# Second head's keys in the weight buffers, parked loads and half rows placed anew, first output norms one tile later: a two-layer hybrid trunk on one Trainium2 core

## The chip, the cores and the metric

One core of one Trainium2 chip runs the whole program. The metric is the device time in microseconds (us) from launch to end; the median of three runs of the kernel before is 3038.08 us, and the runs lie between 3037.23 and 3039.92. The traces come from one further execution, taken by the hardware profiler. Engines are named as in the profile: PE (TensorE matmul), DVE (VectorE), ACT (ScalarE), POOL (GpSimd), SP (SyncE, whose queue issues most of the DMAs).

## The reference, cut to what matters

Two layers run over 256 context tokens and then over 1024 latent tokens with the same weights. Each layer computes, in float32:

```
h  = rms_norm(x) * (1 + sc1) + sh1
p_pool, p_q, p_k, p_v, p_uv = split(h @ w_in)
y_a = multiscale_pool(p_pool) @ w_pool
y_b = for 4 heads: (softmax(q1 k1^T/8) - lam * softmax(q2 k2^T/8)) @ v, then rms_norm per head
y_c = chunked gating of p_uv
x  = x + g1 * (concat(y_a, y_b, y_c) @ w_out)
h2 = rms_norm(x) * (1 + sc2) + sh2
gate, up = split(h2 @ w_ffn_in)
x  = x + g2 * ((silu(gate) * up) @ w_ffn_out)
```

The modulations sh, sc and g are silu(cond) @ w_ada. Latent queries see 256 cached keys and 1024 own ones, so 1280 keys a head; context queries see the 256 context keys.

## The kernel before, in words

All 1280 tokens stand as three column chunks (`CH`): chunk 0 is the 256 context tokens, chunks 1 and 2 are 512 latent tokens each. A float32 product is made of three float32r matmuls, for which each operand is split into a rounded high part and a remainder: `split` (L107 to L109) casts on ACT and subtracts on DVE. Weights come from HBM by a DMA on SP's queue into a raw tile (`raw_slab`, L102 to L105, two buffers), and the two parts land in one of **four weight buffers** (`wtile`, L114). A list of loads in the order of use (`want`, `fetch`, `load_w`) says which weight comes next; `fetch(n)` issues loads and splits until n tiles are ready.

PE's order is the order of the program everywhere. The other engines' order is made by the framework's planner, with its own costs and priorities, so a load or a DVE instruction can be put earlier than its line; only the latent attention is ordered by hand on every engine (`man`, L917 to L1037).

**Latent attention** (L963 to L1036) goes through 32 query tiles of 128 tokens, j = 0 to 31, eight for each of the four heads, with three more turns to drain. A turn makes the two score products of tile j (`s0`, `s1`, L397), their row maxima on DVE (`m0`, `m1`, L401), the exponentials on ACT (`e0`, `e1`, L404), and the transposes (L932) and value products (L415) of earlier tiles. At the first tile of a head, `load_q` brings its queries and `load_kb` (L811 to L821) its keys: four tiles of 1280 columns, two DMAs each, all on SP's queue. The pool of these tiles has five buffers, so one tile of a new head can be loaded ahead and three have to wait for the last tile of the old head. In the first tile of a head (`new`, L999) the transposes and the first value product stand before the second score product, elsewhere they stand inside and behind it. Four of the coming output weights are fetched at j = 5, 8, 11 and 14 (L1033), each with one cast on ACT and one subtraction on DVE in the hand-written order. During head 0 the four weight buffers hold at first the query weights and then head 0's values (one buffer).

**The output product** (`w_out`, L1075) multiplies the mixed rows with the output weights. Its part for chunk 0 needs only what is ready; those for chunks 1 and 2 need the attention's rows scaled by their norms, which `mix_out` does (L1082): four multiplications on DVE (L433), four transposes on PE (L438), a copy on ACT and a subtraction on DVE. In the kernel before, two `mix_out` stand behind each of the four `w_out(0, m)` (L1089 to L1091).

**The FFN** multiplies the 22 slabs of `w_ffn_in` with chunks 1 and 2 as a two by two block product with seven instead of eight half products (`seven`, L1292). For five slabs (1 to 5, `PRE`) the first two of them are made beforehand, parked in HBM (`FS`), and read back by `kept` (L1285); `five` (L1330) makes the other five. Seven-product and five-product slabs alternate (`AFTER`, L42). The sums of weights that the scheme needs are made on POOL (L156 to L169). Between the products, `ada_after` issues half rows of `w_ada` (`ada_half`, L280): one DMA on SP's queue into one of two buffers, and two reductions on DVE (L286) placed behind a marked instruction. Tiles for copies (`cp`), for gates (`g`) and for half rows (`ra`) have three, three and two buffers.

The order at a five-product slab is

```
product(pa_, quarter(s24, 0), t2)
V.tensor_add(u2, p1, pa_)               # L1336
product(pc, quarter(s31, 1), t1)
V.tensor_add(u3, p1, pc)                # L1340
product(pa_, quarter(s31, 0), t3, False)
```

so PE's third product, which writes on into `pa_`, waits until L1336 has read it.

Of the kernel before, what the change touches and what calls it, by code (L numbers as in the profile page):

```python
# [19 lines left out]
P = 128  # L20
# [3 lines left out]
SEQ = 256  # L24
# [25 lines left out]
def build(tc, d):  # L50
# [13 lines left out]
    def nm(s):  # L64
        uid[0] += 1
        return f"{s}_{uid[0]}"
# [475 lines left out]
    for l in range(DEPTH):  # L542
# [265 lines left out]
        kx = ExitStack()  # L808
        kp = opened(kx, "kp", side="right")

        def load_kb(pool, h, k0, n, tag, bufs):  # L811
            kb = []
            for m in range(2):
                row = []
                for i in range(2):
                    t = pool.tile([P, n], F32R, tag=tag, bufs=bufs, name=nm("kb"))
                    for r in range(2):
                        ld(t[r * 64:(r + 1) * 64], KS[l][i, h, m * 64:(m + 1) * 64, k0:k0 + n])
                    row.append(t)
                kb.append(row)  # L820
            return kb  # L821
# [141 lines left out]
        for j in range(NQ + 3):  # L963
            if j < NQ:
                h, i = divmod(j, 8)
                if i == 0:
                    aq = load_q(h, SEQ)
                    kb = load_kb(kp, h, SEQ, NKEY, "kb", 5)
                    box = {}
                elif i % 2 == 0:  # L970
                    aq = aq_next
                if i % 2 and i < 7:
                    aq_next = load_q(h, SEQ + (i + 1) * P)
                if j == 2:
                    open_rest()
                if i == 0:
                    if j == 0:
                        wt = wp.tile([P, 2, 1024], F32R, tag="w", bufs=4, name=nm("vt"))
                        vt = [wt[:, x, :5 * P].bitcast(F32).rearrange("p (a e) -> p a e", e=P) for x in range(2)]
                    else:  # L980
                        vt = [boxes["bp"].tile([P, 5, P], F32, tag="vt", bufs=3, name=nm("vt")) for _ in range(2)]
                    box["vt"] = vt
                    hc = slice(h * P, (h + 1) * P)
                    for x, n, src in ((0, 2, d["cv"][l, :, hc]), (2, 3, VS[l][SEQ:SEQ + 3 * P, hc]),
                                      (5, 5, VS[l][SEQ + 3 * P:, hc])):
                        nc.gpsimd.dma_start(vt[x // 5][:, x % 5:x % 5 + n],
                                            src.rearrange("(a p) e -> p a e", p=P))
                if (j and i == 0) or j == 2:
                    box["o"] = boxes["bo"].tile([P, 8, P], F32, tag="o", bufs=NH - 1, name=nm("o")) \
                        if h < NH - 1 else op.tile([P, 8, P], F32, tag="o", name=nm("o"))  # L990
                    o_all.append(box["o"])
                if j > 2 and mix_ld:
                    c, y = mix_ld.pop(0)
                    t0, n = CH[c]
                    for x in range(2):
                        nc.gpsimd.dma_start(mix[c][:, x, (0, 1, 6, 7)[y]].bitcast(F32),
                                            MS[l].bitcast(F32)[x, y, :, t0:t0 + n])
                tiles[j] = dict(h=h, i=i, kb=kb, aq=aq, box=box, st=stt[:, h], E=[])
            new = j < NQ and j % 8 == 0 and j > 0  # L999
            piece(j, "s0")  # L1000
            piece(j, "m0")
            if j != 1 and j != 2:
                piece(j - 1, "e1")
            piece(j - 3, "v2")
            piece(j - 3, "out")
            piece(j - 2, "t0")
            piece(j - 2, "c0")
            if j != 1 and j != 2:
                piece(j - 1, "comb")
            if new or j >= NQ:  # L1010
                piece(j - 2, "t1")
                piece(j - 2, "c1")
                piece(j, "e0")
                piece(j - 2, "v0")
                piece(j, "s1")
                piece(j, "m1")
            else:
                piece(j, "s1")
                piece(j - 2, "c1")
                piece(j, "e0")  # L1020
                piece(j, "m1")
                piece(j - 2, "v0")
            piece(j - 2, "t2")
            piece(j - 2, "c2")
            piece(j - 2, "v1")
            if j < 2:
                late()
                piece(j, "e1")
                piece(j, "comb")
                late = qk_step(ws, True, 2, 2 + j, psum())  # L1030
            if j == 1:
                late()
            if j in (5, 8, 11, 14):  # L1033
                fetch(j // 3)
            if j in (3, 5):
                ctx_out(j // 2 - 1)  # L1036
        man.close()  # L1037
# [44 lines left out]
        def mix_out(c, h):  # L1082
# [2 lines left out]
            out_norm(l, o_all[h][:, b * 4:b * 4 + 4],  # L1085
                     mix[c][:, 0, 2 + h], mix[c][:, 1, 2 + h])

        ws = load_w(4)
        for m in range(4):  # L1089
            w_out(0, m, ws[m])  # L1090
            mix_out(1 + m // 2, 2 * (m % 2))  # L1091
            mix_out(1 + m // 2, 2 * (m % 2) + 1)
        ab.close()
        fa = ExitStack()
        ntb[0] = 3
# [39 lines left out]

        for c in (1, 2):
            for m in range(4):
                w_out(c, m, ws[m])
                if c == 2:
                    fetch(m + 1)  # L1140
                ada_halves(2)
# [150 lines left out]
        def seven(f, wg, pa_, p1, s24, wh, rest, more, ctx, lead):  # L1292
            first = not callable(rest)
            if lead:
                g1 = product2(wg, p1)
            product(pa_, quarter(s24, 0), t2, False)
            u2 = copied(pa_)
            if not lead:
                g1 = product2(wg, p1)
            if ctx:  # L1300
                pg = ctx_gate(wg)
            a21, s31 = (None, rest) if first else rest()
            pc = fpsum(512)
            product(pc, quarter(s31, 1), t1)
            product(pa_, quarter(s31, 0), t3, False)
            u3 = copied(pa_)
            nxt = product1(load_w(1, 1)[0]) if more else None
            mark = V.tensor_add(u3, u3, pc)
            if ctx:
                ada_after(mark, 1)  # L1310
            if ctx and not more:
                ctx_up((a21, wh), f, pg)
            product(pa_, wh, t4, False)
            mark = V.tensor_mul(g1, g1, pa_)  # L1314
            keep_ft(f, 1, g1)
            ada_after(mark, 1)
            if ctx and more:
                ctx_up((a21, wh), f, pg)
            fetch(1)
            product(pc, quarter(s24, 1), b22, False)  # L1320
            g2 = gtile()
            V.tensor_add(g2, u2, pc)
            S.activation(g2, g2, AF.Silu)
            mark = V.tensor_mul(g2, g2, u3)
            keep_ft(f, 2, g2)
            ada_after(mark, 1)
            return nxt


        def five(f):  # L1330
            s24, wh = load_w(1, 1)[0]
            p1, g1 = kept(f, 2, "cp"), kept(f, 1, "g")
            pa_, pc = fpsum(512), fpsum(512)
            product(pa_, quarter(s24, 0), t2)
            u2 = fpa.tile([P, 512], F32, tag="cp", bufs=3, name=nm("pc"))
            V.tensor_add(u2, p1, pa_)  # L1336
            s31 = load_w(1, 1)[0]
            product(pc, quarter(s31, 1), t1)
            u3 = fpa.tile([P, 512], F32, tag="cp", bufs=3, name=nm("pc"))
            V.tensor_add(u3, p1, pc)  # L1340
            product(pa_, quarter(s31, 0), t3, False)
            ada_after(V.tensor_add(u3, u3, pa_), 1)
            product(pc, quarter(s24, 1), b22, False)
            g2 = gtile()
            V.tensor_add(g2, u2, pc)
            S.activation(g2, g2, AF.Silu)
            V.tensor_mul(g2, g2, u3)
            keep_ft(f, 2, g2)
            fetch(1)
            product(pa_, quarter(wh, 0), t4, False)  # L1350
            V.tensor_add(p1, p1, pa_)
            V.tensor_mul(g1, g1, p1)
            keep_ft(f, 1, g1)

        s24, s31 = load_w(2, 2)
        seven(FIRST - 1, *product1(w[0]), s24, quarter(w[1], 1), s31, False, False, True)
        nxt = None
        for f, g in zip(AFTER, AFTER[1:] + (None,)):
            if f in PRE:
                five(f)  # L1360
                continue
            lead = nxt is None
            if lead:
                nxt = product1(load_w(1, 1)[0])
            s24, wh = load_w(1, 1)[0]

            def rest():
                return load_w(2, 2)

            nxt = seven(f, *nxt, s24, quarter(wh, 0), rest, g is not None and g not in PRE, f >= FIRST, lead)  # L1370
# [210 lines left out]
```

## Time and profile before

| | |
|---|---|
| median of three runs | 3038.08 us |
| the profiled execution's own time | 3045.66 us |
| its span, first to last instruction | 3043.9 us |
| PE busy | 2917.2 us, 96% of the span |
| DVE, ACT, POOL busy | 1997.3, 1110.9, 687.8 us |
| mean granted TensorE clock | 0.986 of full speed |

PE is the bound of nearly all of the span. What can be saved by a change that leaves the products as they are is the time in which PE waits or runs slower, so the places at which it waits are what is to be read. A time "[1.35 <-DMA kb<-KS]" behind an instruction of the trace is the engine's idle time before it and what ended it.

### The profile page before, as it was taken

The numbers are of one execution on the slowest core, as the hardware profiler recorded it, in microseconds if no ns is written. First come the engines' busy times: TensorE is split into PE (matmuls) and PEld (weight loads), VectorE is DVE, ScalarE is ACT, GpSimd is POOL, SyncE is SP. The second block draws the span as 40 slices with busy tenths as digits, with TensorE's granted clock in tenths as the row PEclk, the third lists the DMA queues.
The fourth block names the chain that finished last, engine by engine and source line by source line (L and its number), as shares of the span: only waits on it lengthen the run. The fifth ranks groups of instructions, "written<-read, shape, count | busy, mean of one in ns | idle before, by whom it ended". The sixth has DMA issues, their size and how long they took to land.

```text
span 3043.9 us, 41519 instructions
## 1 busy us (share of the span) xinstructions
PE 2917.2 (96%) x15800; PEld 2500.7 (82%) x15800; DVE 1997.3 (66%) x3221; ACT 1110.9 (36%) x1887; POOL 687.8 (23%) x756
## 2 busy tenths in 40 slices
PE   7999899999999999999989998999999999999997
PEld 4888788888778888888877887888878888888886
DVE  5777777666665554776768767766866533347767
ACT  4423577254222323211252236761632222231112
POOL 1222300035433332000112222000454433310002
PEclk9999999999999999999999999999999999999998
DMA  6476632533333233521235665424433322152211
GB/s 227 152 219 186 190 94 54 180 130 119 120 121 111 94 99 106 189 94 67 77 111 162 209 171 170 115 88 145 138 116 127 101 68 68 68 195 94 94 63 70
DMA packets 155959, 380.65 MB, mean 125 GB/s; under 512 B 20320, under 2 KB 52336, under 8 KB 155504
## 3 DMA queue, kind: packets, MB, share of 16 engines
q1 hardware_dynamic: 111232, 274.00, 28.6%
q0 software_dynamic: 44240, 103.84, 10.1%
q8 instruction: 124, 2.03, 0.3%
q14 instruction: 75, 0.61, 0.1%
q10 hardware_dynamic: 288, 0.16, 0.0%
HBM read 281.97 MB, written 95.95 MB: 124 GB/s over the span
## 4 chain that ended last, share of the span: by engine, by line
PE 78%; DVE 10%; DMA 4%; issue 3%; ACT 3%; POOL 1%; SPq 0%; DVEq 0%; POOLq 0%; ACTq 0%
PE f L217 33%; PE f L1242 24%; PE pa L217 6%; PE pa L457 4%; PE S L397 4%; PE ps L415 4%; PE ps L932 2%; DMA kb<-KS 2%; DVE w L109 1%; DVE ps L286 1%; DVE stt L401 1%; ACT E L404 1%; DVE ps L274 1%; ACT w L108 1%; DMA raw<-w_adaT 1%
## 5 line engine op out<-in xcount | busy, mean ns | idle before, releaser
L217 PE MATMUL f<-ft,w 128*128 128x512 f32 (+1 forms) x3168 | 615.0, 356 | 0.0
L217 PEld LDWEIGHTS f<-ft,w 128*128 128x128 f32 x3168 | 524.8, 190 | 86.8
L108 ACT CAST w<-raw 128x1024 fp32r<-128x1024 f32 x246 | 254.2, 1049 | 723.0 <-PE f L217 410.4
L1242 PE MATMUL f<-h,w 128*128 128x512 f32 x2112 | 506.9, 391 | 1.1 <-ACT pc L1190 1.1
L109 DVE TENSOR_TENSOR w<-raw,w 128x1024 fp32r<-128x1024 f32 x246 | 307.6, 1259 | 295.9 <-ACT w L108 295.5
L1242 PEld LDWEIGHTS f<-h,w 128*128 128x128 f32 x2112 | 392.8, 188 | 82.7 <-ACT pc L1190 1.9
L1072 DVE SCALAR_TENSOR_TENSOR x<-f,mod,x 128x512 f32<-128x512 f32 (+1 forms) x544 | 340.8, 653 | 168.8 <-PE f L217 165.1
L1242 PE MATMUL f<-T,w 128*128 128x512 f32 x1080 | 265.9, 395 | 19.7 <-DVE pc L1336 16.8
L1242 PEld LDWEIGHTS f<-T,w 128*128 128x128 f32 x1080 | 202.4, 188 | 69.9 <-DVE pc L1336 20.8
L217 PE MATMUL pa<-h,w 128*128 128x512 f32 (+1 forms) x1296 | 249.8, 353 | 0.8 <-DVE vn L635 0.8
L401 DVE TENSOR_REDUCE stt<-S 128x1 f32<-128x1280 f32 x128 | 189.8, 1487 | 76.1 <-PE S L397 76.1
L217 PEld LDWEIGHTS pa<-h,w 128*128 128x128 f32 x1296 | 212.6, 192 | 32.5 <-DVE vn L635 1.0
L316 POOL TENSOR_TENSOR nacc<-nacc,room 128x512 f32<-128x512 f32 (+1 forms) x45 | 51.3, 1140 | 799.1 <-ACT room L315 742.3
L457 PE MATMUL pa<-w,h 128*128 128x512 f32 x912 | 220.0, 399 | 11.2 <-DVE w L109 10.7
L217 PE MATMUL f<-mix,w 128*128 128x512 f32 (+1 forms) x1152 | 225.7, 356 | 0.0
L397 PE MATMUL S<-kb,aq 128*128 128x512 f32 (+1 forms) x768 | 198.9, 384 | 19.0 <-DMA kb<-KS 11.7
L457 PEld LDWEIGHTS pa<-w,h 128*128 128x128 f32 x912 | 172.9, 192 | 52.6 <-DVE w L109 8.7
L217 PEld LDWEIGHTS f<-mix,w 128*128 128x128 f32 x1152 | 190.9, 190 | 29.5
L1183 POOL DMA_DIRECT2D FS<-sg x132 | 73.1, 554 | 568.2 <-DVE sg L1314 227.8
L415 PE MATMUL ps<-vt,pt 128*128 128x128 f32 x1280 | 180.7, 282 | 5.9 <-ACT pt L938 5.9
L404 ACT ACTIVATE E<-S,stt 128x1280 f32<-128x1280 f32 x128 | 170.5, 1332 | 38.8 <-DVE stt L401 38.8
L217 PEld LDWEIGHTS f<-h,w 128*128 128x128 f32 x1392 | 172.7, 192 | 3.3
(230 smaller groups left out, 3928.0 us busy)
## 6 DMA issues: line engine op xcount, KB each, us to landing
raw<-w_fi SPq DMA_DIRECT2D x112, 512.0 KB, 3.7
ft<-FS SPq DMA_DIRECT2D x44, 640.0 KB, 5.1
ra<-w_adaT SPq DMA_DIRECT2D x96, 256.0 KB, 2.9
FS<-sg POOLq DMA_DIRECT2D x88, 256.0 KB, 2.3
raw<-w_fo SPq DMA_DIRECT2D x44, 512.0 KB, 5.3
kb<-KS SPq DMA_DIRECT2D x64, 320.0 KB, 6.4
raw<-w_adaT SPq DMA_DIRECT2D x32, 512.0 KB, 4.2
raw<-w_in SPq DMA_DIRECT2D x20, 512.0 KB, 3.6
```

What stands on the lines that cost most here:

```text
L108: S.copy(hi, src)
L109: V.tensor_sub(lo, src, hi.bitcast(F32))
L217: PE.matmul(ps, lhsT=a, rhs=b, start=(i == 0), stop=(i == n - 1))
L397: PE.matmul(ps[:, o:o + n], lhsT=aq[:, m, q0:q0 + P], rhs=kb[m][1 - p][:, o:o + n], start=(p == 0), stop=(p == 1))
L401: V.reduce_max(st[:, m:m + 1], ps[:, :nkey], axis=AX.X, negate=True)
L404: S.activation(E, ps[:, :nkey], AF.Exp, bias=st[:, m:m + 1], accum_out=st[:, 2 + m:3 + m])
L415: PE.matmul(o[:, :P], lhsT=pt[:, i * P:(i + 1) * P], rhs=vt(b + i), start=(b + i == 0), stop=(b + i == nk - 1))
L457: PE.matmul(ps, lhsT=a[:, y], rhs=wk[:, z], start=(k == 0 and x == 0), stop=(k == KD - 1 and x == 2))
L932: PE.transpose(T_["tp", b][:, x * P:(x + 1) * P], T_["E"][0][:, (4 * b + x) * P:(4 * b + x + 1) * P], ident)
L1072: V.scalar_tensor_tensor(xs[c][:, m], in0=ps, scalar=mods[l][:, g0 + m, COND[c]:COND[c] + 1], in1=xs[c][:, m], op0=ALU.mult, op1=ALU.add)
L1183: nc.gpsimd.dma_start(FS[l][f, :, t0:t0 + n], sg)
L1242: PE.matmul(ps, lhsT=y, rhs=z, start=(first and i == 0), stop=(i == 11), skip_group_check=not first)
```

## The change

The second head's keys (h = 1) take one tile from the keys' pool and three from the weight buffers. The fetches of the output weights move from j = 5, 8, 11, 14 to j = 25, 27, 29, 31. The `mix_out` pairs start behind `w_out(0, 1)` instead of `w_out(0, 0)`, and `w_out(1, 0)` is made before the last pair. In the FFN the parked values of a coming five-product slab are asked for inside the seven-product slab ahead of it (`keep_next`), the half row at the end of such a slab moves to the end of the five-product slab, and the first product of the next slab is made before the five-product slab's last product.

```diff
-        def load_kb(pool, h, k0, n, tag, bufs):
+        def load_kb(pool, h, k0, n, tag, bufs, own=4):
...
-                    t = pool.tile([P, n], F32R, tag=tag, bufs=bufs, name=nm("kb"))
+                    if 2 * m + i < own:
+                        t = pool.tile([P, n], F32R, tag=tag, bufs=bufs, name=nm("kb"))
+                    else:
+                        t = wtile().rearrange("p a b -> p (a b)")[:, :n]
...
-                    kb = load_kb(kp, h, SEQ, NKEY, "kb", 5)
+                    kb = load_kb(kp, h, SEQ, NKEY, "kb", 5, 1 if h == 1 else 4)
...
-            if j in (5, 8, 11, 14):
-                fetch(j // 3)
+            if 24 < j < 32 and j % 2:
+                fetch((j - 23) // 2)
...
+        left = [(c, h) for c in (1, 2) for h in range(NH)]
+
+        def mix_two():
+            for _ in range(min(2, len(left))):
+                mix_out(*left.pop(0))
+
         ws = load_w(4)
         for m in range(4):
             w_out(0, m, ws[m])
-            mix_out(1 + m // 2, 2 * (m % 2))
-            mix_out(1 + m // 2, 2 * (m % 2) + 1)
+            if m:
+                mix_two()
+        w_out(1, 0, ws[0])
+        mix_two()
         ab.close()
...
             for m in range(4):
-                w_out(c, m, ws[m])
+                if (c, m) != (1, 0):
+                    w_out(c, m, ws[m])
...
             if ctx and more:
                 ctx_up((a21, wh), f, pg)
+            if not more:
+                keep_next(f)
             fetch(1)
             product(pc, quarter(s24, 1), b22, False)
...
             keep_ft(f, 2, g2)
-            ada_after(mark, 1)
+            ada_after(mark, int(more))
             return nxt
+
+        parked = {}
+
+        def keep_next(f):
+            g = dict(zip((FIRST - 1,) + AFTER, AFTER)).get(f)
+            if g in PRE:
+                parked[g] = kept(g, 2, "cp"), kept(g, 1, "g")
...
-            p1, g1 = kept(f, 2, "cp"), kept(f, 1, "g")
+            p1, g1 = parked.pop(f)
...
             keep_ft(f, 2, g2)
-            fetch(1)
+            nxt = product1(load_w(1, 1)[0])
             product(pa_, quarter(wh, 0), t4, False)
             V.tensor_add(p1, p1, pa_)
-            V.tensor_mul(g1, g1, p1)
+            mark = V.tensor_mul(g1, g1, p1)
             keep_ft(f, 1, g1)
+            ada_after(mark, 1)
+            return nxt
...
             if f in PRE:
-                five(f)
+                nxt = five(f)
                 continue
```

## Rows read from the trace of the kernel before

**Rows 1.** The page: shares of the chain that ended last, by engine.

```profile
PE 78%; DVE 10%; DMA 4%; issue 3%; ACT 3%; POOL 1%; SPq 0%; DVEq 0%; POOLq 0%; ACTq 0%
```

**Rows 2.** Timeline of DVE, layer 0: start us, us, instruction [idle before, releaser].

```profile
368.55 1.49 DVE L401 TENSOR_REDUCE stt<-S 128x1 f32<-128x1280 f32 x1 [0.84 <-PE S L397]
...
393.50 1.49 DVE L401 TENSOR_REDUCE stt<-S 128x1 f32<-128x1280 f32 x1 [0.87 <-PE S L397]
...
423.70 1.48 DVE L401 TENSOR_REDUCE stt<-S 128x1 f32<-128x1280 f32 x1
...
445.46 1.49 DVE L401 TENSOR_REDUCE stt<-S 128x1 f32<-128x1280 f32 x1 [0.87 <-PE S L397]
...
494.55 1.49 DVE L401 TENSOR_REDUCE stt<-S 128x1 f32<-128x1280 f32 x1 [0.99 <-PE S L397]
...
523.06 1.49 DVE L401 TENSOR_REDUCE stt<-S 128x1 f32<-128x1280 f32 x1 [0.90 <-PE S L397]
```

**Rows 3.** The same timeline of DVE, layer 1.

```profile
1870.33 1.49 DVE L401 TENSOR_REDUCE stt<-S 128x1 f32<-128x1280 f32 x1 [0.82 <-PE S L397]
...
1891.19 1.49 DVE L401 TENSOR_REDUCE stt<-S 128x1 f32<-128x1280 f32 x1 [0.50 <-PE S L397]
...
1921.77 1.48 DVE L401 TENSOR_REDUCE stt<-S 128x1 f32<-128x1280 f32 x1
...
1941.58 1.49 DVE L401 TENSOR_REDUCE stt<-S 128x1 f32<-128x1280 f32 x1 [1.03 <-PE S L397]
```

**Rows 4.** Timeline of PE: head 1 in layer 0, head 2 in layer 1.

```profile
381.28 2.47 PE L397 MATMUL S<-kb,aq 128*128 128x512 f32 x6 [3.08 <-DMA kb<-KS]
...
1926.40 1.40 PE L397 MATMUL S<-kb,aq 128*128 128x512 f32 x6 [0.57 <-ACT pt L938]
...
1932.01 1.43 PE L397 MATMUL S<-kb,aq 128*128 128x512 f32 x6 [1.35 <-DMA kb<-KS]
```

**Rows 5.** Timeline of SP's queue, layer 0: the issues of head 1's keys.

```profile
360.60 11.47 SPq L100 DMA_DIRECT2D kb<-KS  x8
```

**Rows 6.** Timeline of PE: start of the output product, layer 0, then layer 1.

```profile
542.34 1.61 PE L438 MATMUL ps<-ident,o 128*128 128x128 f32 x8 [2.34 <-DVE o L433]
...
546.66 1.03 PE L438 MATMUL ps<-ident,o 128*128 128x128 f32 x8
...
2039.48 1.94 PE L438 MATMUL ps<-ident,o 128*128 128x128 f32 x8 [2.05 <-DVE o L433]
2041.07 3.91 PE L217 MATMUL f<-mix,w 128*128 128x256 f32 x24
```

**Rows 7.** Line L1336: who waited for it (total us, times).

```profile
  PE f L1242: 16.8, 9
```

**Rows 8.** Timeline of PE, third product of three of the five-product slabs.

```profile
860.38 4.30 PE L1242 MATMUL f<-T,w 128*128 128x512 f32 x12 [2.02 <-DVE pc L1336]
...
2398.55 3.06 PE L1242 MATMUL f<-T,w 128*128 128x512 f32 x12 [1.34 <-DVE pc L1336]
...
2437.41 3.04 PE L1242 MATMUL f<-T,w 128*128 128x512 f32 x12
```

**Rows 9.** Timeline of DVE about the first five-product slab, layer 0.

```profile
775.16 1.77 DVE L1324 TENSOR_TENSOR sg<-sg,pc 128x512 f32<-128x512 f32 x1
776.85 0.75 DVE L286 CUSTOM_DVE_ANT_0 ps<-ra,condh,cols 128x512 f32<-128x512 f32 x1
...
777.52 0.68 DVE L1336 TENSOR_TENSOR pc<-kt,f 128x512 f32<-128x512 f32 x1
...
788.15 0.69 DVE L1352 TENSOR_TENSOR kt<-kt,kt 128x512 f32<-128x512 f32 x1
794.29 1.23 DVE L109 TENSOR_TENSOR w<-raw,w 128x1024 fp32r<-128x1024 f32 x1 [5.46 <-ACT w L108]
```

**Rows 10.** Timeline of PE: the last product of that slab.

```profile
783.88 2.96 PE L1242 MATMUL f<-T,wh 128*128 128x512 f32 x12
```

**Rows 11.** Timeline of ACT: the next copy of a first product.

```profile
789.63 0.59 ACT L1190 COPY pc<-f 128x512 f32<-128x512 f32 x1 [2.12 <-PE f L1242]
```

## The prediction, made before the change was run

> **What bounds the kernel.** I read the page first. Of the chain that ended last, 78% is PE, and DMA and ACT have 4% and 3% [rows 1]. The products stay as they are, so the change can pay only where PE waits. The table of waits and the rows of PE with idle time then lead to three places: the first tile of a head in the latent attention, the start of the output product, and the third product of a five-product slab. For the attention I use the maxima of the first score product (L401) as a clock, one per query tile: between tiles 26 and 31 of layer 0, five tiles take 523.06 - 494.55 = 28.51, that is 5.70 a tile [rows 2]. What a stretch takes above that is what the reader is to see there.
>
> All terms come from the profiled execution, which took 3045.66 us (span 3043.9), 0.25% over the median of 3038.08. I take differences from it and subtract them from the median.
>
> **Keys of the second head.** At head 1 of layer 0, tiles 7 to 10 take 393.50 - 368.55 = 24.95 against 3 x 5.70 = 17.10, so 7.85 are lost. At head 2, tiles 15 to 18, 445.46 - 423.70 = 21.76 loses 4.66 [rows 2]. In layer 1 the same stretches take 20.86 and 19.81, losses of 3.76 and 2.71 [rows 3]. The sum is 18.98. PE waits there for the key DMAs, and the six score matmuls run in 2.47 instead of 1.40 in the worst case [rows 4]. The cause is on SP's queue: it reaches the eight key DMAs of head 1 at 360.60, some 8 us before tile 7's maxima at 368.55, and then stays at them for 11.47, since six of the eight must wait for the old head's tiles [rows 2, 5].
>
> With three tiles in the weight buffers none of the eight waits. The buffers are idle then: query weights are done with tile 1, and nothing else is fetched before j = 25. At some 0.6 a DMA (PE's wait ended at 381.28, while the issue ended at 372.07, so landing took 9.2 under load [rows 4, 5]) the last is issued at about 365.4 and landed by 374.6. That is before the second score product of tile 8, which came at 381.28 before and would come some 6 us after tile 8's first one. The query DMAs behind them on SP come earlier too. Head 2 gains likewise: head 1 takes only the fifth buffer of the keys' pool, so all four that head 2 needs are free from tile 8 on. Head 3 stays as it is, since three of its four buffers are head 2's.
>
> What stays of these losses is the order of a head's first tile, with its second score product behind the transposes. Head 2 of layer 1 shows it best: of 2.71 lost, waits of 1.35 and 0.57 are the keys' (the second is put down to ACT, but stands before the first score product, which needs a key tile that waited) [rows 3, 4]. That leaves 0.8. The bounds are 0 and 2.71; I take 0.8, from the boundary with the smallest wait in it. Gain: 18.98 - 4 x 0.8 = **15.8**.
>
> **Fetches.** Each puts a cast into ACT's hand-written order and a subtraction into DVE's. From tile 10 to 15 of layer 0, with two fetches, 30.20 pass instead of 28.51 [rows 2]: 0.84 each. Before, three per layer cost this, and the fourth (j = 8) lay in the boundary counted above. After, all four stand in full tiles, the last just ahead of the drain, where it delays an exponential that three more turns wait for. Price: 0.84 more per layer, **-1.7** in all; bounds 0 and, if the drain takes the last fetch twice and none recovers, -3.4. The raw loads keep their place in SP's order ahead of need, as their two buffers are free all through the attention; nothing waits behind them but queries, which come two tiles ahead.
>
> **Output product.** Before the first transposes PE waits 2.34 in layer 0 and 2.05 in layer 1 for the multiplications by the norms. The transposes then take 1.61 and 1.94 where later ones take 1.03, and in layer 1 the product behind them takes 3.91, some 0.8 over its kind, which runs about 3.1 [rows 6]. Together 2.9 + 3.8 = 6.7. Now `w_out(0, 1)`, 3.1 long, stands before the first transposes and covers a wait of 2.3. If DVE puts that product's own addition ahead of the multiplications, about 1 per layer comes back. `w_out(1, 0)` needs chunk 1 alone, whose four norms are done one product earlier. The pools close some 2 us later, and with them the first half rows; before the change nothing of PE waited for those. Bounds 0 and 6.7; taken **6.6**.
>
> **Five-product slabs.** PE waits for L1336 nine times, 16.8 in all [rows 7]: seven times 2.02 and twice 1.34 (one row of each stands), and at the tenth slab, where no half rows are left, not at all [rows 8]. In the first slab a half row's reduction of 0.75 stands right ahead of L1336 [rows 9]. The change takes it away from there: 777.52 - 776.85 = 0.67, which is also 2.02 - 1.34 less a rounding, and the layer 1 slab with 1.34 indeed has none there. Seven slabs by 0.67 give **4.7**. Bounds 0 and 16.8. The half row goes behind L1352, where DVE is idle for 5.46 [rows 9], so its two reductions are covered there; without that cover they would cost up to their length, 1.8 a slab. The parked loads only move earlier on SP's queue. If one found no free buffer it would hold the raw loads and half rows behind it, but three copies' buffers are free in turn by then. The first product of the next slab moves one product ahead; PE loses nothing if its weights are split by then. The bounds are 0 and one product, 2.96 a slab [rows 10]; I take 0, since no row of PE shows a wait for a split here.
>
> A rule speaks to what is left, by itself: the Trainium skill, SBUF - State Buffer, section "Who interferes with whom", says that a DVE instruction with two SBUF inputs and a GpSimd instruction that reads SBUF exclude one another on a shared port, one of them blocked outright. By that rule the trace agrees: L1324 takes 1.77 next to POOL's sums, L1352 of the same shape 0.69 [rows 9]. As the sums' place against these subtractions may shift with the change, it makes the second rival possible.
>
> **Sum:** 15.8 - 1.7 + 6.6 + 4.7 = 25.4, so 3038.1 - 25.4 = **3012.7 us**. A measurement of this kernel can tell about 0.2%, 6.1 us, from no change.
>
> **Rivals.**
> *The fives' wait vanishes.* If the slow DVE instructions ahead of L1336 shrink to 0.69 or go behind it, the nine remaining waits of 1.34 go too, 12.1 more: 3000.6. For it: the tenth slab has none. Against: the one with no half row at its front still has 1.34 [rows 8].
> *The heads keep more.* If the boundary costs 2.71 even with keys in place, and fetches cost their upper bound, the attention gives 8.1 - 3.4 = 4.7 instead of 14.1: 3022.1. For it: one wait there is put down to ACT [rows 4].
> *The change doesn't do what it says.* If SP doesn't bring the keys earlier, because something else holds the queue at head 1, only the other terms stay: 6.6 + 4.7 - 1.7 = 9.6, so 3028.5. Against: SP is at these DMAs at 360.60 already [rows 5].
> *Slower: the fourth copy's buffer.* The next slab's first product is now copied while the parked value, u2 and u3 hold all three `cp` buffers. If the planner gives the copy the parked value's buffer, it waits for L1352, which ends at 788.84, while PE is through the slab's last product at 786.84 [rows 9, 10]; with the copy's 0.59 [rows 11] PE waits 2.6 before the next slab's second product, and after such a wait twelve matmuls can take 4.30 instead of 3.06 [rows 8]. Ten slabs by 2.6 to 3.8 are 26 to 38, and 3012.7 becomes 3039 to 3051, in the middle 3045. From 3.2 a slab on it is slower by over 0.2%. Against: u2 is free earlier, and a planner takes what is free first.
>
> **Chances.** The forecast 0.58, the fives' wait vanishing 0.10, heads keeping more 0.12, keys not earlier 0.10, the copy's buffer 0.06, and 0.04 for a mixture that ends level. The range goes from 3000 (the second case, and the boundary at nothing) to 3029 (keys not earlier). Faster by over 0.2%, below 3032: 0.58 + 0.10 + 0.12 and most of 0.10, 0.87; within 0.2%: 0.08; slower: 0.05.
>
> **What would show it.** Right: no wait for keys on PE at heads 1 and 2, and the same at head 3; tiles 7 to 10 in about 18; SP through the eight DMAs in about 5; no idle time before L438; waits of 1.34 behind L1336. Wrong: waits of PE for a copy (L1190) at the slabs, tiles 25 to 31 longer by more than 3 in sum, transposes waiting for L433 again, or key waits that last.

## The result and the profile after

The changed kernel takes 3012.85 us (median of six runs, 3009.85 to 3015.41), the kernel before 3037.65 in the same comparison (six runs, 3030.57 to 3041.68): the ratio is 0.9920, with a 95% interval of 0.9907 to 0.9933, or 24.3 us less (20 to 28). The forecast was 3012.7. The profiled execution took 3014.92, with a span of 3013.1.

Where the 30.8 us between the two spans lie is seen from the first matmul of each stage. Each column is the time from one such start to the next, worked out from the timelines of PE.

| us | layer 0: scores to output product | to the first T product | to the second FFN product | layer 1: scores to output product | to the first T product | to the second FFN product | the rest |
|---|---|---|---|---|---|---|---|
| before | 224.24 | 193.90 | 491.28 | 219.92 | 194.93 | 486.14 | 1233.49 |
| after | 214.70 | 191.20 | 486.24 | 214.59 | 190.94 | 484.73 | 1230.70 |
| less | 9.54 | 2.70 | 5.04 | 5.33 | 3.99 | 1.41 | 2.79 |

So 14.9 are in the latent attention, 6.7 in the output product, 6.5 in the FFN. The last 2.8, of which 2.74 are ahead of layer 0's scores, are in code that the change doesn't touch, and other runs of the same code differ by as much.

Not all of it is waiting that went away. By the pages, PE's busy time for the same 15,800 matmuls fell from 2917.2 to 2907.3 us, while the mean granted TensorE clock rose from 0.986 to 0.989. By the profile's windows, 7.7 of these 9.9 lie in the six stretches of the table. So about a third of the 30.8 is matmuls that run faster, and the rest is shorter waits. How the two hang together is seen at the slabs and in the last section.

**Attention.** The timeline of DVE, layer 0, the maxima that serve as a clock (they answer to [rows 2]):

```profile
364.53 1.49 DVE L401 TENSOR_REDUCE stt<-S 128x1 f32<-128x1280 f32 x1 [0.97 <-PE S L397]
...
382.35 1.49 DVE L401 TENSOR_REDUCE stt<-S 128x1 f32<-128x1280 f32 x1 [1.01 <-PE S L397]
...
410.86 1.49 DVE L401 TENSOR_REDUCE stt<-S 128x1 f32<-128x1280 f32 x1 [0.91 <-PE S L397]
...
428.68 1.49 DVE L401 TENSOR_REDUCE stt<-S 128x1 f32<-128x1280 f32 x1 [1.02 <-PE S L397]
...
457.14 1.49 DVE L401 TENSOR_REDUCE stt<-S 128x1 f32<-128x1280 f32 x1 [0.87 <-PE S L397]
...
480.12 1.49 DVE L401 TENSOR_REDUCE stt<-S 128x1 f32<-128x1280 f32 x1
...
485.40 1.49 DVE L401 TENSOR_REDUCE stt<-S 128x1 f32<-128x1280 f32 x1 [0.49 <-PE S L397]
...
509.90 1.49 DVE L401 TENSOR_REDUCE stt<-S 128x1 f32<-128x1280 f32 x1 [0.48 <-PE S L397]
```

Tiles 7 to 10 take 17.82, and so do tiles 15 to 18: 0.72 over three steady tiles at both heads. Layer 1 has 17.83 and 17.84 there. Head 3 (tiles 23 to 26) takes 22.98 where it took 20.57; it now holds a fetch, and its slow score product below. Tiles 26 to 31 take 29.78, 1.27 over five steady ones. That stretch starts late, since tile 26 is already held up by the fetch at 25. The two whole periods from tile 27 (485.40) to tile 31 (509.90), with one fetch each, take 24.50, 1.69 over four steady tiles.

The timeline of SP's queue at head 1 shows why (it answers to [rows 5]):

```profile
357.10 1.24 SPq L100 DMA_DIRECT2D kb<-KS  x2
358.38 4.85 SPq L100 DMA_DIRECT2D w<-KS  x6
```

The eight key DMAs are through in 6.1 instead of 11.47, with no wait among them; six go to weight buffers (`w`). PE's timeline at heads 1, 2 and 3, then the drain and the start of the output product in layer 0 (answering to [rows 4] and [rows 6]):

```profile
371.90 1.16 PE L415 MATMUL ps<-vt,pt 128*128 128x128 f32 x8 [0.25 <-ACT pt L941]
...
418.22 1.16 PE L415 MATMUL ps<-vt,pt 128*128 128x128 f32 x8 [0.25 <-ACT pt L941]
...
468.28 2.42 PE L397 MATMUL S<-kb,aq 128*128 128x512 f32 x6 [1.50 <-DMA kb<-KS]
...
517.24 0.66 PE L935 MATMUL ps<-ident,E 128*128 128x128 f32 x4 [1.27 <-ACT o L420]
...
524.60 6.00 PE L217 MATMUL f<-mix,w 128*128 128x256 f32 x48
530.43 1.03 PE L438 MATMUL ps<-ident,o 128*128 128x128 f32 x8
```

In the first tiles of heads 1 and 2 PE's only idle time is 0.25 behind the transposes; the key wait is left at head 3 alone, where the score product behind it takes 2.42 instead of 1.40. The drain waits 1.27 for ACT where it waited 0.82 before: the last fetch's cast stands ahead there. From the last tile's maxima to the output product it is 14.70 instead of 13.82. The first transposes of the output product start behind two products without idle time, and at full speed.

**FFN.** The table of waits of PE (engine, line, whom it waited for: total us, times, longest) has the addition of the five-product slabs, L1357 in this kernel, at 12.1 instead of 16.8 [rows 7], each now 1.33 or 1.34:

```profile
PE f L1254 <- DVE pc L1357: 12.1, 9, 1.3
```

The timeline of DVE about the first five-product slab (answering to [rows 9]):

```profile
753.70 0.76 DVE L286 CUSTOM_DVE_ANT_0 ps<-ra,condh,cols 128x512 f32<-128x512 f32 x1
...
756.07 1.78 DVE L286 CUSTOM_DVE_ANT_0 ps<-ra,condh,cols 128x512 f32<-128x512 f32 x1
...
757.78 0.68 DVE L1336 TENSOR_TENSOR sg<-pc,f 128x512 f32<-128x512 f32 x1
758.41 1.80 DVE L109 TENSOR_TENSOR w<-raw,w 128x1024 fp32r<-128x1024 f32 x1
760.14 1.77 DVE L1338 TENSOR_TENSOR sg<-sg,pc 128x512 f32<-128x512 f32 x1
761.84 0.68 DVE L1357 TENSOR_TENSOR pc<-kt,f 128x512 f32<-128x512 f32 x1
```

The half row that stood between the multiplication (L1338, L1324 before) and the addition is gone. Another one, behind the gate's product, is still ahead of all this; its two reductions begin at 753.70 and 756.07.

### The profile page after: what moved, and what is told of

Same layout as the page of the kernel before. It is cut to its first block, busy times and chain, and to the rows that moved or that the text cites. A ratio compares the mean times of both kernels' runs of the same rounds, so it can differ in the third digit from the quotient of the medians.

```text
span 3013.1 us, 41516 instructions
## 1 busy us (share of the span) xinstructions
PE 2907.3 (96%) x15800; PEld 2493.6 (83%) x15800; DVE 2007.3 (67%) x3221; ACT 1108.9 (37%) x1887; POOL 689.2 (23%) x756
## 4 chain that ended last, share of the span: by engine, by line
PE 77%; DVE 11%; issue 4%; ACT 3%; DMA 2%; POOL 2%; SPq 0%; DVEq 0%; POOLq 0%; ACTq 0%
PE f L217 33%; PE f L1254 24%; PE pa L217 6%; PE ps L415 4%; PE S L397 4%; PE pa L457 3%; PE ps L935 2%; DVE stt L401 1%; ACT E L404 1%; DVE w L109 1%; DVE ps L274 1%; DVE E L411 1%; DVE ps L286 1%; DMA raw<-w_adaT 1%; DMA kb<-KS 1%
## 5 line engine op out<-in xcount | busy, mean ns | idle before, releaser
L109 DVE TENSOR_TENSOR w<-raw,w 128x1024 fp32r<-128x1024 f32 x246 | 307.6, 1259 | 269.5 <-ACT w L108 269.1
L1254 PE MATMUL f<-T,w 128*128 128x512 f32 x1080 | 264.8, 394 | 15.0 <-DVE pc L1357 12.1
L217 PE MATMUL f<-h,w 128*128 128x256 f32 x1392 | 174.0, 283 | 0.0
```

The source lines that it names most:

```text
L109: V.tensor_sub(lo, src, hi.bitcast(F32))
L217: PE.matmul(ps, lhsT=a, rhs=b, start=(i == 0), stop=(i == n - 1))
L1254: PE.matmul(ps, lhsT=y, rhs=z, start=(first and i == 0), stop=(i == 11), skip_group_check=not first)
```

## The experiments

All times are medians; "less" and "more" against the kernel before go by the ratio of the runs of one comparison. The changed kernel has 0.9920 (0.9907 to 0.9933).

**Each part alone.** The first takes the hunks of `load_kb` and of the fetches, the second those of `mix_out`, the third those of `seven` and `five`, from the diff above, into the kernel before.

Keys and fetches (label e1_keys_fetch):

> The kernel before with the keys and the fetches of the change alone. Separate terms (theory): 14.1 us less than the kernel before, tiles 7 to 10 and 15 to 18 in about 17.8 us in both layers, the third product of the five-product slabs still waiting 2.02 and the first transposes of the output product still waiting 2.0 to 2.3. Rival, that the three parts only pay together: under 8 us less.

3029.98 against 3037.87; ratio 0.9971 (0.9960 to 0.9982), 8.8 less (5.5 to 12.2). That is less than 14.1, and as the interval reaches below 8, this run alone doesn't exclude the rival; the sum of the three parts below speaks against it. In its trace the attention takes 213.52 and 214.17 from the scores to the output product, as in the changed kernel. Three of the four boundaries take 17.8 to 18.1; tiles 7 to 10 of layer 0 take 18.55, with a wait for a key tile in a weight buffer (the first row below), so these keys are not always in time.

Two things can have made the sum smaller; no run separates them. First, the attention before is not always as long as in the profiled execution on which the forecast rests: the next two kernels, with the same attention, take 221.48 and 221.22 in layer 0 where that one took 224.24. The difference lies at heads 1 and 2: tiles 7 to 10 and 15 to 18 take 46.71 together in that execution, 43.93 and 43.46 in the other two. The granted clock over layer 0's attention is 0.96 in that one, 0.97 and 0.98 in the others. Second, PE still waits 2.0 at the slabs in this kernel, and products behind such a wait can be slow. Its timeline of PE at that key tile and at two slabs of layer 1:

```profile
374.10 1.40 PE L397 MATMUL S<-w,aq 128*128 128x512 f32 x6 [0.50 <-DMA w<-KS]
...
2258.94 4.21 PE L1245 MATMUL f<-T,w 128*128 128x512 f32 x12 [2.00 <-DVE pc L1339]
...
2341.99 4.61 PE L1245 MATMUL f<-T,w 128*128 128x512 f32 x12 [2.00 <-DVE pc L1339]
```

Twelve matmuls take 3.06 elsewhere. Layer 1's five-product part is 489.26 long in this execution against 486.14.

First norms (label e2_first_norms):

> The kernel before with the later first norms alone. Theory: 6.6 us less, no idle time before the first transposes of the output product in either layer, and later half rows cost PE nothing. Rival, that DVE orders the second tile's addition ahead of the multiplications or that the later half rows come back as waits: 0 to 4 us less.

3030.55; ratio 0.9978 (0.9969 to 0.9986), 6.7 less (4.3 to 9.4). As forecast: 191.02 and 191.11 from the output product to the FFN, where the kernel before has 193.90 and 194.93, and the transposes have no idle time before them. The later half rows cost PE nothing.

FFN (label e3_ffn):

> The kernel before with the changes of the FFN alone. Theory: 4.7 us less, up to 6.5 where the slower products behind a wait go too; nine waits of 1.34 us behind the first addition of a five-product slab. Rival, that those waits depend on where the attention ended: another number of waits, or other lengths.

3032.17; ratio 0.9980 (0.9972 to 0.9989), 6.1 less (3.3 to 8.5). Nine waits of 1.3 us, whatever the attention did. The three parts alone sum to 21.6, and together they give 24.3; the difference is within the intervals, and nothing says that the parts pay only together.

**Keys back in their pool** (label e4_keys_in_pool), on the changed kernel:

```diff
-                    kb = load_kb(kp, h, SEQ, NKEY, "kb", 5, 1 if h == 1 else 4)
+                    kb = load_kb(kp, h, SEQ, NKEY, "kb", 5)
```

> The changed kernel with all heads' keys in their own pool again, the fetches still at 25 to 31. Theory (the keys' place pays): 13 to 16 us more than the changed kernel, with PE waiting for keys at heads 1 and 2 again. Rival (it is the fetches that pay, since they leave the boundary of head 1): at most 4 us more.

3028.21; ratio 0.9964 (0.9952 to 0.9976). That is 13 more than the changed kernel by the ratios, 15.4 by the medians, so it is the keys' place that pays and not the fetches'. The timeline of PE has the waits back at heads 1 and 2 of both layers, here head 1 of layer 0 and head 2 of layer 1:

```profile
374.18 1.41 PE L397 MATMUL S<-kb,aq 128*128 128x512 f32 x6 [2.24 <-ACT E L404]
...
379.55 1.40 PE L397 MATMUL S<-kb,aq 128*128 128x512 f32 x6 [1.10 <-DMA kb<-KS]
...
1913.10 1.40 PE L397 MATMUL S<-kb,aq 128*128 128x512 f32 x6 [0.89 <-DMA kb<-KS]
...
1918.76 2.17 PE L397 MATMUL S<-kb,aq 128*128 128x512 f32 x6 [1.40 <-DMA kb<-KS]
```

The row at 374.18 is put down to an exponential; it is the first score product of the head and goes with the keys, since it has no such wait in the changed kernel. The same can be read of [rows 4]'s 0.57.

**The half row back** (label e7_half_row_back), on the changed kernel:

```diff
-            ada_after(mark, int(more))
+            ada_after(mark, 1)
...
             keep_ft(f, 1, g1)
-            ada_after(mark, 1)
             return nxt
```

> The changed kernel with the half row back at the end of the seven-product slab ahead of a five-product slab, and none at that one's end. Theory (that half row's reduction stands right ahead of the addition PE waits for): the waits go back to 2.0 us in seven slabs, 4.7 us more than the changed kernel, and up to 7 where products behind such a wait run slower. Rival (the parked loads or the product's place made the gain): the waits stay at 1.34, the time within 2 us.

3020.72; ratio 0.9949 (0.9936 to 0.9961), 7.9 more than the changed kernel by the medians. Waits of 2.0 in seven slabs, as in the kernel before, and again some products behind them are slow (PE's timeline):

```profile
763.99 4.48 PE L1254 MATMUL f<-T,w 128*128 128x512 f32 x12 [2.01 <-DVE pc L1357]
...
806.61 3.06 PE L1254 MATMUL f<-T,w 128*128 128x512 f32 x12 [2.02 <-DVE pc L1357]
...
2294.84 3.06 PE L1254 MATMUL f<-T,w 128*128 128x512 f32 x12 [1.35 <-DVE pc L1357]
```

**The other two edits of the FFN, undone one by one** on the changed kernel: the first product behind the slab's last one again (e8_first_product_back), and the parked values loaded in the slab again (e12_parked_in_five).

```diff
-            nxt = product1(load_w(1, 1)[0])
+            fetch(1)
             product(pa_, quarter(wh, 0), t4, False)
...
-            return nxt
...
-                nxt = five(f)
+                five(f)
```

> The changed kernel with the first product of the next slab behind the five-product slab's last product again. Theory (this product's place neither pays nor costs): within 2 us of the changed kernel, nine waits of 1.34 behind the first addition. Rival (it shifts POOL's sums against DVE's subtractions): other waits at the slabs, 3 us or more either way.

```diff
-            if not more:
-                keep_next(f)
...
-            p1, g1 = parked.pop(f)
+            p1, g1 = kept(f, 2, "cp"), kept(f, 1, "g")
```

> The changed kernel with the parked values loaded inside the five-product slab again. Theory (those loads were hidden before): within 2 us of the changed kernel, waits of 1.34 behind the first addition. Rival (their place made the gain): waits of 2.0 or more, 5 us more.

3013.51 (ratio 0.9919, 0.9907 to 0.9932) and 3013.18 (0.9918, 0.9906 to 0.9930): neither can be told from the changed kernel's 0.9920, with nine waits of 1.3 in both. Of the FFN's three edits, as the change makes them, only the half row's place is seen to pay.

**What holds the last 1.3 us at a slab?** First the half row behind the gate's product was taken away too (label e5_no_half_row_ahead):

```diff
             mark = V.tensor_mul(g1, g1, pa_)
             keep_ft(f, 1, g1)
-            ada_after(mark, 1)
+            ada_after(mark, int(more))
...
             keep_ft(f, 1, g1)
-            ada_after(mark, 1)
+            ada_after(mark, 2)
             return nxt
```

> The changed kernel without the half row that stands behind the gate's product in a seven-product slab ahead of a five-product slab; two stand at the end of the five-product slab instead. Theory (DVE's backlog sets the 1.34 us that PE still waits, and this half row's two reductions of some 0.8 and 1.8 us are part of it): the nine waits go to nothing, 10 to 12 us less than the changed kernel. Rival (the wait is set by the parked value's load or by POOL's sums, whatever half rows do): the waits stay at 1.3 us, and the time within 2 us of the changed kernel.

3011.36; ratio 0.9918 (0.9903 to 0.9933), the same as the changed kernel. My theory fell and the rival held: the waits are 1.01 at the first slab of a layer and 1.27 to 1.28 at the others. So that no half rows are left does not by itself explain why the tenth slab has no wait [rows 8]; what does is not shown. The timelines of DVE, then ACT, then POOL at the first slab say what took the half row's place:

```profile
755.10 0.69 DVE L1336 TENSOR_TENSOR sg<-pc,f 128x512 f32<-128x512 f32 x1 [1.60 <-DMA FS<-sg]
757.15 1.79 DVE L109 TENSOR_TENSOR w<-raw,w 128x1024 fp32r<-128x1024 f32 x1 [1.36 <-ACT w L108]
758.87 1.77 DVE L1338 TENSOR_TENSOR sg<-sg,pc 128x512 f32<-128x512 f32 x1
760.57 0.68 DVE L1357 TENSOR_TENSOR pc<-kt,f 128x512 f32<-128x512 f32 x1
```

```profile
756.06 1.06 ACT L108 CAST w<-raw 128x1024 fp32r<-128x1024 f32 x1 [3.28 <-POOL raw L158]
```

```profile
754.73 1.30 POOL L158 TENSOR_TENSOR raw<-raw 128x512 f32<-128x512 f32 x1
...
756.55 1.31 POOL L168 TENSOR_TENSOR raw<-raw 128x512 f32<-128x512 f32 x1
757.94 2.16 POOL L169 TENSOR_TENSOR raw<-raw,raw 128x512 f32<-128x512 f32 x1
```

With the backlog gone, DVE idles for 1.36 ahead of the split (L109). The cast before it waits for POOL's sum of the weights (L158), and the split stands ahead of the multiplication (L1338) and of the addition (L1357) in the planner's order. Split and multiplication take 1.79 and 1.77 next to POOL's further sums (L168, L169), where the like take 1.22 and 0.69. By the Trainium skill, SBUF - State Buffer, section "Who interferes with whom", two-input DVE instructions and POOL's reads exclude one another, and the trace agrees with these times; but the rival of the prediction, that these instructions would move apart, did not come. This chain from POOL to the addition is read from the trace; no run takes a link out of it.

So the wait was covered instead of shortened (label e10_product_between), on the changed kernel:

```diff
+            nxt = product1(load_w(1, 1)[0])
             product(pa_, quarter(s31, 0), t3, False)
...
-            nxt = product1(load_w(1, 1)[0])
             product(pa_, quarter(wh, 0), t4, False)
```

> The changed kernel with the first product of the next slab made between the second and the third product of the five-product slab. Theory (DVE's order, with a split that waits for POOL's sum and a multiplication ahead of the addition, makes the addition 1.3 us late, and nothing on PE covers it): 2.7 us of other work cover the wait, nine waits go, 10 to 12 us less than the changed kernel. Rival (the product's weights or its copy come too late): PE waits there instead, the same time or more.

3003.74; ratio 0.9883 (0.9868 to 0.9898), clear of the changed kernel's: 9 less by the medians, 11 by the ratios. PE's timeline at the first slab, then DVE's:

```profile
758.96 2.88 PE L1254 MATMUL f<-T,w 128*128 128x512 f32 x12
761.68 5.60 PE L1254 MATMUL f<-h,w 128*128 128x512 f32 x24
767.12 2.96 PE L1254 MATMUL f<-T,w 128*128 128x512 f32 x12
```

```profile
765.17 0.68 DVE L1357 TENSOR_TENSOR pc<-kt,f 128x512 f32<-128x512 f32 x1
```

The addition is as late as before against the second product: it starts 3.49 behind that product's start here (761.68), 3.50 in the changed kernel (758.34). But PE has the next slab's first product to make until 767.1 and never waits. No five-product slab has idle time in this trace. So it is shown what the wait cost and that it can be covered, not what makes the addition late.

**The fetches elsewhere** (label e6_fetch_18_21_24_27):

```diff
-            if 24 < j < 32 and j % 2:
-                fetch((j - 23) // 2)
+            if j in (18, 21, 24, 27):
+                fetch((j - 15) // 3)
```

> The changed kernel with the output weights fetched at tiles 18, 21, 24 and 27 instead of 25, 27, 29 and 31. Theory (a fetch costs 0.84 in a full tile, nothing in the first tile of head 3, where PE waits for keys, and 0.9 in the drain): 1 to 2 us less than the changed kernel, the drain 0.9 shorter in each layer. Rival (the cast in head 3's first tile delays the tiles behind it): the same time or up to 2 us more, and head 3's first three tiles longer by 0.8.

3011.99; ratio 0.9920 (0.9907 to 0.9932), not told apart from the changed kernel by time. The traces are 2.3 and 1.3 shorter from the scores to the output product (212.43 and 213.32), and the drain waits 0.79 and 0.78 for ACT instead of 1.27, which speaks for the theory without settling its size.

**One tile of head 2 in a weight buffer** (label e9_head2_three_own):

```diff
-                    kb = load_kb(kp, h, SEQ, NKEY, "kb", 5, 1 if h == 1 else 4)
+                    kb = load_kb(kp, h, SEQ, NKEY, "kb", 5, (4, 1, 3, 4)[h])
```

> The changed kernel with one of head 2's four key tiles in a weight buffer too, so that head 3 finds two free tiles in the keys' pool. Theory (what head 3 loses, 4.8 to 5.0 us a layer, is the wait for tiles of the old head): the first score products of head 3 no longer wait, the second wait 0.5 to 1.5 instead of 1.4 to 1.5, 1 to 4 us less than the changed kernel. Rival (the planner gives head 2 a weight buffer that head 1 still holds): head 2 waits instead, the same time or more.

3008.67; ratio 0.9910 (0.9895 to 0.9925): 4.2 less than the changed kernel by the medians, with intervals that overlap. The trace is clear: from the scores to the output product 210.72 and 211.96, 4.0 and 2.6 less, and head 3's first tile has no wait for keys at all, neither at the first score product (462.70) nor at the second (466.75). Why is less clear: SP issues the last of head 3's eight key DMAs at 460.1 in this trace and in the changed kernel's, and the slowest of them took 6.4 to land here and 8.1 there. The rows of layer 0:

```profile
462.70 1.44 PE L397 MATMUL S<-kb,aq 128*128 128x512 f32 x6
...
465.84 1.16 PE L415 MATMUL ps<-vt,pt 128*128 128x128 f32 x8 [0.25 <-ACT pt L941]
466.75 1.41 PE L397 MATMUL S<-kb,aq 128*128 128x512 f32 x6
```

**All three together** (label e11_best): the product between, head 2 with three own tiles, fetches at 18, 21, 24 and 27.

> The product between, head 2 with three tiles of its own and fetches at 18, 21, 24 and 27 together. Theory (the three are separate): 3012.9 less 12 less 4 less 1, about 2996. Rival (head 2's weight buffer holds the last fetch up): a wait in head 3, over 3000.

2994.42; ratio 0.9856 (0.9843 to 0.9870). That is 43.7 less than the kernel before and, by the medians, 18.4 less than the changed one, near the theory's 2996 and under the rival's 3000.

## Why the prediction was right, point by point

*Keys.* The cause is shown: with the keys in their pool again the waits and 13 to 15 us come back. What stays at a head's first tile was forecast at 0.8 and is 0.72 to 0.74 in all four places of the changed kernel's trace. The size of the gain was taken from one execution, and that one was long: its layer 0 attention exceeds those of the two other traces with the same attention code by 2.8 and 3.0. By those two the term of 15.8 was some 3 too large, by the keys put back up to 2.4; and the part alone measured 8.8 (5.5 to 12.2) instead of 14.1 for keys and fetches. Part of what the forecast counted as lost was not waiting: the score product of 2.47 [rows 4] was made at a granted clock of 0.50.

*Fetches.* Forecast 0.84 each and the same in the drain. Between tiles 27 and 31 two cost 1.69 together, 0.85 each; the drain grew by 0.88. The net price of 1.7 is of the right size.

*Output product.* Forecast 6.6; alone 6.7 (4.3 to 9.4), in the traces of before and after 2.70 + 3.99 = 6.7. The transposes have no wait left that DVE's order could have caused.

*Five-product slabs.* The mechanism is shown by the half row put back, and the waits came out at 1.33 to 1.34 as forecast. The term of 4.7 was probably too small: it counted the wait and left out the products that run slower behind a wait of 2.0, although [rows 8] show one. Alone the part gives 6.1 (3.3 to 8.5), by the stages of the traces 6.5, and put back it costs 7.9. The half row's new place is covered: its reductions at the slab's end run in DVE's idle time.

*The sum* was closer than its terms, and that is luck: the errors had opposite signs, up to 3 too much for the keys, 1.4 to 3.2 too little at the slabs. The lower end of the range, 3000, is the fives' wait gone alone (3000.6); with the boundary at nothing as well it would have been 2997.

*Rivals.* The fives' wait did not vanish, and the heads kept 0.72, not 2.71. Keys do arrive earlier. The copy's buffer makes no wait: no five-product slab, and no slab behind one, shows PE waiting for it. The first product's place and the parked loads, costed at nothing, show no effect beyond the intervals when they are undone.

## What to carry to other kernels

A transfer that waits for a buffer of the phase before it can be given a buffer that lies idle in just that phase, even one of another purpose; count who needs it back, and when. Where an in-order engine is late by a microsecond, removing its work may only expose the next dependence in its queue, as the second half row did; putting independent work of the waiting engine into the gap covered the wait here, and the time shows no cost. And a term taken from one profiled execution should be compared with the spread of the runs: the kernel before varied by 11 us over six runs, and three traces of the same attention code by 3.0 in one layer.

## What the runs showed of the hardware that was not expected

Products behind an idle time of PE can be slow, and in the traces these are products for which the granted TensorE clock was lower. In the kernels with waits of 2.0 us at the slabs (before, e1, e2, e7) seven of 28 were followed by twelve matmuls in 4.2 to 4.6 instead of 3.06; of the 80 waits of 1.0 to 1.35 there in all traces not one was. The profile's windows over two of the 28 in the kernel before, one of usual length and the slow one of [rows 8] (the number behind POOL is the granted clock, 1.00 is 2.4 GHz):

```profile
819.31:822.38 3.07, 3.07 (x13) 2.52 (x14) 1.21 (x3) 0.00 (x0) 0.00 (x0) 1.00 0.81 275
860.38:864.68 4.30, 4.29 (x13) 3.40 (x14) 1.22 (x3) 0.00 (x0) 0.00 (x0) 0.67 0.58 205
```

PE had been idle for 2.02 us before either. The first ran at 2.4 GHz throughout; 0.67 for the second means that it ran in part at the lower level, 1.2 GHz. Why the one and not the other, no run shows, and the length of the wait alone doesn't decide it: in the changed kernel's attention the score product behind a wait of 1.50 (468.28) had 0.51 and took 2.42 instead of 1.40.

So shortening a wait from 2.0 to 1.3 gave more than the 0.67 of the wait itself: the seven slow products took 9.7 us more than 7 x 3.06, which over 28 waits is an estimate of 0.34 a wait, or 2.4 for the seven of one run. The runs before vary more than those after, 3030.57 to 3041.68 against 3009.85 to 3015.41, but not for this reason alone: with the half row back and waits of 2.0 (e7) five runs lie within 3020.02 to 3023.10, and with waits of 1.3 in the kernel before (e3) twelve lie between 3026.30 and 3037.12. What makes the kernel before vary is not shown.
